# Moving the up projection's weight sums to GpSimd, its Relu and Square to VectorE, and three units' row transfers to GpSimd's queue

## The chip, the cores and the metric

The kernel runs on one core of a Trainium2 chip. The metric is the device time of one execution in microseconds (us). Before the change the median of three runs is 2260.8 us (2259.25 to 2261.42).

## What is computed

One layer of a decoder block on x of shape 1 x 1024 x 1024 in float32. Two token mixers (dilated windowed attention and retention) read the normalised input through one projection, are gated, added, projected (`w_out`) and added to x. Then comes the channel mixer, which the change touches:

```
xn2 = rmsnorm(x, norm2_g)
x   = x + square(relu(xn2 @ w_up)) @ w_down      # w_up 1024 x 4096, w_down 4096 x 1024
```

## The kernel before, in words

**Number format.** Every float32 operand is split into two float32r parts: ScalarE copies it, rounded, into the high part (line 351), and VectorE subtracts that from the original for the low part (line 352). A product takes three matmuls for each pair of tiles: high by high, low by high, high by low (lines 253 to 259).

**The up projection** (lines 1195 to 1311) goes over 16 units j of 256 columns of `w_up`. Each unit is computed by a seven-product scheme of Strassen's kind: products N1 to N7, each of four contractions by three matmuls of 128 x 512, in an order written out by `strassen_order` (line 287): for unit j N6, N5, then N1 of unit j+2, N7, N3, then N2 of unit j+2, N4. `product` (line 400) issues one of them and takes its result away. N6, N7 and N4 accumulate in one and the same bank, whose running content is copied out between them: line 424 (ScalarE) after N6, line 429 (VectorE) after N7.

**The results.** `result` (line 1210) gets the four quarters of a unit's output. Two come in PSUM (`q11`, `q12`, after N2 and N4), two as tiles in SBUF (`u3` after N7, `u2` after N3, made by the subtractions of lines 429 and 434). Each goes through Relu and Square on ScalarE (lines 1219 and 1220). Sums of them (line 1227, VectorE) are the seven operands of the down projection; `put_operand` splits each into a tile `hs` (four buffers) and stores it to `h_d` in HBM from SyncE's queue (line 1237).

**The weights** of a unit come in two raw tiles (line 207, SyncE's queue), of which there are four places: units j and j+2 share theirs. `add_units` (line 125) lists the steps that make the split pieces: A (both halves of the second raw tile) for N1 and N2, D (half of the first) for N4, then the four sums of lines 148 to 151 in the raw tiles on VectorE, then B (second tile) for N6 and N3, C (first tile) for N5 and N7. The list runs A of unit j+1, D, sums, B and C of unit j, then A of unit j+2, and so on. A step is written into the program (`pump`, line 211) as soon as the products that last used its buffer are in it, and a raw tile is loaded anew as soon as the step that used it last (B for the second tile, C for the first) is written.

**The handover.** The operand tiles N1, N5 and N3 of the up projection become the buffers for the rows of `h_d` that the down projection multiplies (`load_rows`, line 1246): a pair of transfers, `xh` and `xl`, of 896 KB each, for every unit u of 32. The rows of u = 0, 1 and 2 are asked for while the last up unit (j = 15) still runs, right after its N1, N5 and N3; all go through SyncE's queue (line 1253). `down` (line 1256) issues the products of the down projection; at the very end GpSimd adds the results into `out` by accumulating transfers (line 1284).

**Order.** Only PE's order is written by hand (line 303). For the other engines and queues a planner sets the order when the program is built: among the instructions that it expects to be ready it takes the one written first. Each engine then works through its list in that order and waits where an operand isn't there. GpSimd's other work is small: row scales (line 366), four-tile differences at the start (line 547), some scalings in attention (line 678).

Of the kernel before, what the change touches and what calls it, by code (L numbers as in the profile page):

```python
# [10 lines left out]
F = mybir.dt.float32  # L11
R = mybir.dt.float32r
AF = mybir.ActivationFunctionType
OP = mybir.AluOpType
# [23 lines left out]
class Weights:  # L38
# [83 lines left out]

                    self.steps.append((self.claim(buf, key), r[need, p], step))

    def add_units(self, tag, srcs):

        base = len(self.src)
        kept = {}
        for s in srcs:
            self.place += [(len(self.src) + i - base) % (self.RAW + 1) for i in range(2)]  # L130
            self.src += [s[0], s[1]]

        def piece(key, buf, r, cols, then=None):
            def step():
                if isinstance(buf, tuple):
                    if not kept:
                        kept["D"] = self.buffer(buf[0])
                    h, l = (x[:, 512 * buf[1]:512 * buf[1] + 512] for x in kept["D"])
                else:
                    h, l = self.buffer(buf)  # L140
                self.split(h, l, self.raw[r][:, cols])
                self.units[key] = h, l
                if then:
                    then()

            self.steps.append((self.claim(buf, key), r, step))

        def sums(r):
            (x22, x21), (x11, x12) = ((self.raw[i][:, 0:512], self.raw[i][:, 512:1024]) for i in (r, r + 1))
            for x, y in ((x22, x21), (x21, x11), (x11, x22), (x12, x11)):  # L150
                self.nc.vector.tensor_tensor(x, x, y, op=OP.add)  # L151

        both = slice(0, 1024)
        for j in range(-1, len(srcs)):
            if j + 1 < len(srcs):
                r = base + 2 * (j + 1)
                piece((tag, j + 1, "A"), self.A[(j + 1) % 2], r + 1, both)
            if j >= 0:
                r = base + 2 * j
                piece((tag, j, "D"), (self.D, j % 2), r, slice(0, 512), lambda r=r: sums(r))  # L160
                piece((tag, j, "B"), self.B[j % 2], r + 1, both, lambda r=r: self.used.add(r + 1))
                piece((tag, j, "C"), self.C, r, both, lambda r=r: self.used.add(r))
        m = len(srcs)
        self.cycle = (0, 1, self.B[m % 2], self.C, self.D, self.B[(m - 1) % 2])
        self.turn = 0
# [135 lines left out]
def hybrid_block(ctx: ExitStack, tc: tile.TileContext, a: dict, out: bass.AP):  # L301
# [72 lines left out]
    for u in range(4):  # L374
# [2 lines left out]
    W.add_tokens("att", [[[a["w_att_q"][u, q, p] for p in range(2)] for q in range(4)] for u in range(len(TOKEN))])  # L377
    NG, NQ = KT, 2 * RH
    W.add_units("in", [a["w_gate_q"][j] for j in range(NG)] + [a["w_rqk_q"][j] for j in range(NQ)]
                + [a["w_gr_q"][j] for j in range(8)])  # L380
    for h in range(RH):
        for u in range(4):
            W.add(a["w_rv"][h, u])
# [6 lines left out]
        for u in range(4):  # L390
            W.add(a["w_out"][nb, u], (4, 5, 2, 3)[u] if nb else (2, 3, 0, 1)[u])
    NU = FF // 256
    W.add_units("up", [a["w_up"][j] for j in range(NU)])
    NC = FF // 512
    W.add_chunks("dn", [[a["w_down"][c, i] for i in range(4)] for c in range(NC)],
                 [{"N1": 0, "N2": 1, "N3": 2, "N5": "n2a", "N7": "n2b", "N6": 5, "N4": 4},
# [798 lines left out]
    with ExitStack() as ph:  # L1195
        up_pool, early, sumst = None, [], ExitStack()
        unit = {}

        def temps():

            nonlocal up_pool
            if up_pool is None:
                assert pipe.slot > last_turn
                norm2.close()
                y0 = pool(sumst, "y0", 1)
                Y.update({r: y0.tile([P, D], F, name=f"Y{r}") for r in (0, 4)})
                up_pool = pool(ph, "p26", 2)
            return up_pool

        def result(j, f, cs, src):  # L1210

            if pipe.slot <= last_turn:
                early.append((j, f, cs, src))
                return
            while early:
                result(*early.pop(0))
            q = "u3" if f and cs.start else "u2" if cs.start else ("q11", "q12")[f]
            r = src if src.space != PSUM else temps().tile([P, 512], F, name=q, bufs=2 if f else 3)
            nc.scalar.activation(r, src, AF.Relu)
            nc.scalar.activation(r, r, AF.Square)  # L1220
            held[j, q] = r
            if q != "u2":
                put_operand(j, {"q11": "N1", "q12": "N2", "u3": "N4"}[q], r)
            sums = {"u2": (("N5", "u3", "u2"), ("N7", "u2", "q11"), ("N6", "q11", "u3")),
                    "q12": (("N3", "q12", "q11"),)}.get(q, ())
            for name, x, y in sums:
                nc.vector.tensor_tensor(held[j, x], held[j, x], held[j, y], op=OP.add)
                put_operand(j, name, held[j, x])

        held = {}  # L1230

        def put_operand(j, name, x):

            hs = temps().tile([P, 2, 512], R, name="hs", bufs=4)
            split(hs[:, 0], hs[:, 1], x)
            dst = h_d[j // 2, :, :, :, DOWN.index(name), j % 2]
            nc.sync.dma_start(dst.rearrange("h t p q -> p (h t) q"),
                              hs.rearrange("p h (t q) -> p (h t) q", q=P).bitcast(F))


        units = [(c, t) for c in range(NC) for t in range(4)]
        rows = {}
        sums = {}
        Y = {}

        def load_rows(u):

            if u < len(units):
                c, t = units[u]
                rows[u] = []  # L1250
                for i, x in enumerate(OP7[("N1", "N5", "N3")[u % 3]]):
                    x = x.rearrange("p a b -> p (a b)")[:, :7 * 2 * P]
                    nc.sync.dma_start(x.bitcast(F), h_d[c, i, t].rearrange("p o k q -> p (o k q)"))
                    rows[u].append(x.rearrange("p (o k q) -> p o k q", o=7, k=2))

        def down(u, name):

            c, t = units[u]
            b = sums.setdefault(u, {})
            bank = BANK[name]  # L1260
            fresh = bank not in b
            if fresh:
                b[bank] = mm.tile([P, 512], F, name="mm")
            o = DOWN.index(name)
            wh, wl = W["dn", c, name]
            xh, xl = rows[u]
            pipe.step(b[bank], [(xh[:, o, k], xl[:, o, k], wh[:, 512 * k:512 * k + 512], wl[:, 512 * k:512 * k + 512])
                                for k in range(2)], None, fresh)
            ps = b[bank]
            lo, hi = halves()  # L1270
            if name == "N1":
                b["b"] = ms.tile([P, 512], F, name="ms")
                nc.scalar.activation(b["b"], ps, AF.Copy, scale=-1.0)  # L1273
            else:
                r, ns, op, last = {"N2": (t, lo, OP.add, True), "N6": (t, hi, OP.subtract, False),
                                   "N5": (t + 4, hi, OP.subtract, False), "N7": (t + 4, hi, OP.add, True),
                                   "N3": (t, hi, OP.add, True), "N4": (t + 4, lo, OP.add, True)}[name]
                begun = c > 0 or name in ("N7", "N3")
                if not begun:
                    nc.scalar.activation(Y[r][:, ns], ps, AF.Copy, scale=1.0 if op == OP.add else -1.0)  # L1280
                else:
                    nc.vector.tensor_tensor(Y[r][:, ns], Y[r][:, ns], ps, op=op)
                if last and c == NC - 1:
                    nc.gpsimd.dma_start(out[r * P:(r + 1) * P, ns], Y[r][:, ns], accum_op=OP.add)
            if t == 3:
                W.free(("dn", c, name))

        for j, name in strassen_order(NU):
            product("up", j, name, unit, OP7, temps, result)
            if j == NU - 1:  # L1290
                if name == "N1":
                    load_rows(0)
                if name == "N2":
                    parts = [x.rearrange("p a b -> p (a b)") for x in OP7[name]]
                    for i, part in enumerate("ab"):
                        W.places["n2" + part] = [x[:, 1024 * i:1024 * i + 1024] for x in parts]
                    W.free(("place", "n2"))
                if name == "N5":
                    load_rows(1)
                if name == "N7":  # L1300
                    down(0, "N1")
                if name == "N3":
                    load_rows(2)
                    down(0, "N2")
        exts.close()
        y1 = pool(sumst, "y1", 1, "right")

        Y.update({r: y1.tile([P, D], F, name=f"Y{r}") for t in (1, 3, 2) for r in (t, t + 4)})
        for x in "abc":
            W.places["y1" + x] = [y1.tile([P, UW], R, name=f"y1{x}{i}") for i in "hl"]  # L1310
        W.free(("place", "y1"))
# [122 lines left out]
```

## Time and profile before

| | before |
|---|---|
| median of the runs (lowest, highest) | 2260.8 us (2259.25, 2261.42) |
| the profiled execution, its span | 2260.28 us, 2258.5 us |
| ScalarE's splits of weight pieces, 128 x 1024, 1680 to 1900 | 1.05 us each |
| VectorE's subtractions of weight pieces, 128 x 1024, 1680 to 1900 | 1.22 us each |
| VectorE's weight sums, 128 x 512 (line 151) | 0.69 us each, 160 in all, 64 of them in the up projection |
| ScalarE's Relu and Square in SBUF (lines 1219, 1220; u) | 32 each, 20.0 and 20.2 us |
| loads of raw weight tiles, 1680 to 1900, issue to landing | 5.1 us in the median |
| row transfers of the down projection (line 1253), issue to landing | 6.4 us in the median |

The page of the profile gives busy times for the whole span; a view by stages gives the same for any stretch, and the view of waits tells who waited for whom. A timeline row has the start, the busy time, engine, line, output and inputs; in square brackets how long the engine sat idle just before and what ended that. In rows of one source line, three durations in ns are the shortest, the median and the longest. Engines: PE is TensorE's matmul, DVE is VectorE, ACT is ScalarE, POOL is GpSimd, SP is SyncE; a q behind the name means the engine's queue of transfers.

### The profile page before, as it was taken

The numbers are of one execution on the slowest core, as the hardware profiler recorded it, in microseconds if no ns is written. First come the engines' busy times: TensorE is split into PE (matmuls) and PEld (weight loads), VectorE is DVE, ScalarE is ACT, GpSimd is POOL, SyncE is SP. The second block draws the span as 40 slices with busy tenths as digits, with TensorE's granted clock in tenths as the row PEclk, the third lists the DMA queues.
The fourth block names the chain that finished last, engine by engine and source line by source line (L and its number), as shares of the span: only waits on it lengthen the run. The fifth ranks groups of instructions, "written<-read, shape, count | busy, mean of one in ns | idle before, by whom it ended". The sixth has DMA issues, their size and how long they took to land.

```text
span 2258.5 us, 28527 instructions
## 1 busy us (share of the span) xinstructions
PE 2189.5 (97%) x10064; PEld 1794.3 (79%) x10064; DVE 1432.1 (63%) x2543; ACT 1103.3 (49%) x1934; POOL 194.1 (9%) x180
## 2 busy tenths in 40 slices
PE   8999999999999999989999999999999999899998
PEld 6788788888888887878888788888787777688887
DVE  6766676455655666557867741544867778676863
ACT  6433453577744477545545522113666667522210
POOL 3314453000000000000000000000000000000002
PEclk9999999999999999999999999999999999999999
DMA  6443534454555445455333583553388779966657
GB/s 197 131 126 112 150 93 123 154 161 146 172 151 166 153 151 162 127 177 153 119 89 115 165 284 126 187 177 134 109 232 229 231 225 284 313 243 249 244 221 172
DMA packets 346559, 392.77 MB, mean 174 GB/s; under 512 B 34737, under 2 KB 271921, under 8 KB 346162
## 3 DMA queue, kind: packets, MB, share of 16 engines
q1 hardware_dynamic: 344114, 386.77, 54.7%
q0 software_dynamic: 2304, 4.20, 1.3%
q8 instruction: 79, 1.29, 0.2%
q14 instruction: 62, 0.51, 0.1%
HBM read 252.39 MB, written 138.51 MB: 173 GB/s over the span
## 4 chain that ended last, share of the span: by engine, by line
PE 71%; DVE 8%; DMA 8%; ACT 6%; issue 4%; POOL 3%; SPq 0%; POOLq 0%; ACTq 0%; DVEq 0%
PE mm L254 41%; PE ms L254 24%; DMA raw<-in_w_up 2%; ACT wh L351 2%; DVE wl L352 2%; DMA h_d<-hs 2%; PE tr L787 1%; PE tr L806 1%; DVE raw L151 1%; DVE hs L352 1%; DMA xl<-h_d 1%; POOL x L547 1%; DMA raw<-in_w_att_q 1%; DVE xl L352 1%; PE tr L645 1%
## 5 line engine op out<-in xcount | busy, mean ns | idle before, releaser
L352 DVE TENSOR_TENSOR wl<-raw,wh 128x1024 fp32r<-128x1024 f32 (+1 forms) x292 | 332.4, 1139 | 231.5 <-ACT wh L351 229.8
L351 ACT ACTIVATE wh<-raw 128x1024 fp32r<-128x1024 f32 (+1 forms) x292 | 287.1, 986 | 321.3 <-PE ms L254 110.5
L254 PE MATMUL mm<-xh,wh 128*128 128x512 f32 x896 | 346.3, 410 | 0.0
L254 PE MATMUL mm<-xl,wh 128*128 128x512 f32 x896 | 329.0, 390 | 1.7 <-DVE xl L352 1.7
L254 PE MATMUL mm<-xh,wl 128*128 128x512 f32 x768 | 300.7, 392 | 0.0
L254 PE MATMUL mm<-wh,xh 128*128 128x512 f32 x736 | 297.8, 405 | 2.3 <-ACT ms L1273 2.3
L254 PE MATMUL mm<-wh,xl 128*128 128x512 f32 x736 | 289.3, 393 | 4.0 <-DMA xl<-h_d 4.0
L254 PE MATMUL mm<-wl,xh 128*128 128x512 f32 x736 | 288.0, 391 | 0.0
L254 PE MATMUL ms<-xh,wh 128*128 128x512 f32 x544 | 228.2, 419 | 15.3 <-ACT u L424 13.4
L254 PE MATMUL ms<-xl,wh 128*128 128x512 f32 x544 | 213.6, 393 | 0.7 <-DVE xl L352 0.7
L254 PE MATMUL ms<-xh,wl 128*128 128x512 f32 x544 | 213.6, 393 | 0.0
L254 PEld LDWEIGHTS mm<-xh,wh 128*128 128x128 f32 x896 | 168.9, 189 | 32.5 <-ACT u L427 0.4
L254 PEld LDWEIGHTS mm<-xl,wh 128*128 128x128 f32 x896 | 169.0, 189 | 31.6 <-DVE xl L352 2.1
L254 PEld LDWEIGHTS mm<-xh,wl 128*128 128x128 f32 x768 | 144.3, 188 | 31.4
L254 PEld LDWEIGHTS mm<-wh,xl 128*128 128x128 f32 x736 | 138.9, 189 | 35.3 <-DMA xl<-h_d 4.9
L254 PEld LDWEIGHTS mm<-wh,xh 128*128 128x128 f32 x736 | 139.2, 189 | 28.8 <-ACT ms L1273 3.2
L254 PEld LDWEIGHTS mm<-wl,xh 128*128 128x128 f32 x736 | 139.5, 189 | 26.0
L254 PE MATMUL ms<-wh,xh 128*128 128x512 f32 x336 | 137.1, 408 | 6.7 <-DVE c L700 4.4
L254 PEld LDWEIGHTS ms<-xh,wh 128*128 128x128 f32 x544 | 102.9, 189 | 40.8 <-ACT u L424 18.5
L254 PE MATMUL ms<-wh,xl 128*128 128x512 f32 x336 | 132.8, 395 | 2.5 <-DVE xl L352 2.5
L254 PE MATMUL ms<-wl,xh 128*128 128x512 f32 x336 | 132.3, 394 | 1.0 <-DVE ss L365 0.8
L254 PEld LDWEIGHTS ms<-xh,wl 128*128 128x128 f32 x544 | 102.7, 189 | 22.5
(282 smaller groups left out, 3809.9 us busy)
## 6 DMA issues: line engine op xcount, KB each, us to landing
h_d<-hs SPq DMA_DIRECT2D x112, 512.0 KB, 5.6
xh<-h_d SPq DMA_DIRECT2D x32, 896.0 KB, 4.9
xl<-h_d SPq DMA_DIRECT2D x32, 896.0 KB, 6.9
raw<-in_w_att_q SPq DMA_DIRECT2D x48, 512.0 KB, 4.3
raw<-in_w_up SPq DMA_DIRECT2D x32, 512.0 KB, 5.0
raw<-in_w_down SPq DMA_DIRECT2D x32, 512.0 KB, 5.2
qk_d<-T SPq DMA_DIRECT2D x48, 256.0 KB, 3.5
raw<-in_w_gate_q SPq DMA_DIRECT2D x16, 512.0 KB, 4.5
```

The lines of the kernel that those rows point to most:

```text
L151: self.nc.vector.tensor_tensor(x, x, y, op=OP.add)
L254: self.nc.tensor.matmul(ps, x, y, start=start, stop=stop, skip_group_check=not first)
L351: nc.scalar.activation(dst_h, src, AF.Copy)
L352: nc.vector.tensor_tensor(dst_l, src, dst_h.bitcast(F), op=OP.subtract)
L547: nc.gpsimd.tensor_tensor(x[v], x[v], x[u], op=op)
L645: nc.tensor.transpose(pt[:, i, :], c[:, i * P:(i + 1) * P], ident)
L787: nc.tensor.matmul(sp[:, :w], q[:, e * P:(e + 1) * P], k[:, k0 * P:k0 * P + w], start=True, stop=True)
L806: nc.tensor.matmul(po[:, :DH], st["t"][:, j * P:(j + 1) * P], v[:, k0 + j, :], start=(j == 0), stop=(j == nk - 1))
```

## The change

The weight sums of the up projection are issued on GpSimd (those of the input projection stay on VectorE). Results that are in SBUF (`u2` and `u3`) get Relu and Square from one VectorE instruction, max(r, 0) * r, in place; those in PSUM stay with ScalarE. The row transfers of the first three down units are issued from GpSimd's queue instead of SyncE's.

```diff
-    def add_units(self, tag, srcs):
+    def add_units(self, tag, srcs, adder):
...
             for x, y in ((x22, x21), (x21, x11), (x11, x22), (x12, x11)):
-                self.nc.vector.tensor_tensor(x, x, y, op=OP.add)
+                adder.tensor_tensor(x, x, y, op=OP.add)
...
-                + [a["w_gr_q"][j] for j in range(8)])
+                + [a["w_gr_q"][j] for j in range(8)], nc.vector)
...
-    W.add_units("up", [a["w_up"][j] for j in range(NU)])
+    W.add_units("up", [a["w_up"][j] for j in range(NU)], nc.gpsimd)
...
-            nc.scalar.activation(r, src, AF.Relu)
-            nc.scalar.activation(r, r, AF.Square)
+            if src.space != PSUM:
+                nc.vector.scalar_tensor_tensor(r, src, 0.0, src, op0=OP.max, op1=OP.mult)
+            else:
+                nc.scalar.activation(r, src, AF.Relu)
+                nc.scalar.activation(r, r, AF.Square)
...
-                    nc.sync.dma_start(x.bitcast(F), h_d[c, i, t].rearrange("p o k q -> p (o k q)"))
+                    (nc.gpsimd if u < 3 else nc.sync).dma_start(x.bitcast(F), h_d[c, i, t].rearrange("p o k q -> p (o k q)"))
```

## The prediction

> **What bounds the kernel now.** I read the page's busy shares first, then the stages, then the waits of the one stage that the change touches, then one pass of that stage on each engine.
>
> ```profile
> span 2258.5 us, 28527 instructions
> PE 2189.5 (97%) x10064; PEld 1794.3 (79%) x10064; DVE 1432.1 (63%) x2543; ACT 1103.3 (49%) x1934; POOL 194.1 (9%) x180
> 1680.00:1900.00 220.00, 209.08 (x904) 169.54 (x902) 163.70 (x228) 145.57 (x236) 0.00 (x0) 0.99 0.83 238
> 1900.00:1960.00 60.00, 53.52 (x220) 42.45 (x219) 42.51 (x55) 37.52 (x60) 0.00 (x0) 0.94 1.02 329
> ACT wh L351 <- DMA raw<-in_w_up: 42.9, 10, 5.7
> PEld ms L254 <- ACT u L424: 15.1, 10, 2.6
> PE ms L254 <- ACT u L424: 10.8, 9, 2.2
> ```
>
> TensorE is busy 97% of the span, so the change can only take or give the rest. In the stage table (PE first, then PEld, DVE, ACT, POOL, the granted clock, the DMA share) the up projection loses 220 - 209.1 = 10.9 us of PE between 1680 and 1900, and its handover to the down projection 6.5 us up to 1960. GpSimd stands idle there. The waits from 1680 to 1900 say that all of PE's loss has one releaser, ScalarE's copy of line 424, nine times. ScalarE itself waits ten times for a weight load, 4.3 us each. One pass shows why; ScalarE first, then PE, VectorE and SyncE.
>
> ```profile
> 1751.52 1.06 ACT L351 ACTIVATE wh<-raw 128x1024 fp32r<-128x1024 f32 x1 [4.08 <-DMA raw<-in_w_up]
> ...
> 1759.93 0.62 ACT L351 ACTIVATE wh<-raw 128x512 fp32r<-128x512 f32 x1
> ...
> 1764.70 1.06 ACT L351 ACTIVATE wh<-raw 128x1024 fp32r<-128x1024 f32 x1 [1.62 <-DVE raw L151]
> ...
> 1771.54 1.06 ACT L351 ACTIVATE wh<-raw 128x1024 fp32r<-128x1024 f32 x1 [3.80 <-DMA raw<-in_w_up]
> ```
> ```profile
> 1761.61 0.50 PE L254 MATMUL ms<-xh,wh 128*128 128x512 f32 x1 [0.95 <-ACT u L424]
> ```
> ```profile
> 1752.61 1.23 DVE L352 TENSOR_TENSOR wl<-raw,wh 128x1024 fp32r<-128x1024 f32 x1 [3.56 <-ACT wh L351]
> 1753.76 0.68 DVE L434 TENSOR_TENSOR u<-mm,u 128x512 f32<-128x512 f32 x1
> 1754.46 0.69 DVE L352 TENSOR_TENSOR hs<-u,hs 128x512 fp32r<-128x512 f32 x1
> 1755.80 0.69 DVE L1227 TENSOR_TENSOR u<-u,u 128x512 f32<-128x512 f32 x1 [0.65 <-ACT u L1220]
> ...
> 1760.59 0.69 DVE L352 TENSOR_TENSOR wl<-raw,wh 128x512 fp32r<-128x512 f32 x1 [0.24 <-ACT wh L351]
> 1761.31 0.69 DVE L151 TENSOR_TENSOR raw<-raw 128x512 f32<-128x512 f32 x1
> 1762.04 1.42 DVE L151 TENSOR_TENSOR raw<-raw,raw 128x512 f32<-128x512 f32 x2
> 1763.38 0.68 DVE L352 TENSOR_TENSOR hs<-q,hs 128x512 fp32r<-128x512 f32 x1
> 1763.98 0.68 DVE L151 TENSOR_TENSOR raw<-raw 128x512 f32<-128x512 f32 x1
> ...
> 1765.79 1.23 DVE L352 TENSOR_TENSOR wl<-raw,wh 128x1024 fp32r<-128x1024 f32 x1 [0.52 <-ACT wh L351]
> ```
> ```profile
> 1767.04 0.34 SPq L207 DMA_DIRECT2D raw<-in_w_up  x1
> ```
>
> Read them as a **ring of four legs**, from one split of a weight piece A to the next. Leg a: from A's split at 1751.52 through VectorE's work up to the end of D's split (1760.59 + 0.69 = 1761.28), 9.76 us. Leg b: the four weight sums, until B's split begins at 1764.70, 3.42 us. Leg c: B's split, to 1767.02, 2.32 us. Leg d: only now is that raw tile free, the load goes out at 1767.04 and lands at 1771.54, 4.52 us. Together 20.02 us. PE needs less for a unit: seven products of twelve matmuls, at 904 matmuls in 209.1 us of busy time 84 x 0.2313 = 19.4 us (an estimate from that row, a little high, since records can be missing). So the ring sets the pace. PE feels it through line 424: N7 accumulates into the bank that line 424 must first have copied, and that copy stands in ScalarE's queue behind A's split.
>
> **The change, part by part.** The sums of leg b go to GpSimd. Its only big two-input additions here are those of line 547, of the same shape.
>
> ```profile
> L547 POOL TENSOR_TENSOR x<-x,x x16: 1258/1454/2235, 21.5 to 71.2; 128x512 f32<-128x512 f32 x16
> ```
> ```profile
> 38.94 4.68 POOL L547 TENSOR_TENSOR x<-x,x 128x512 f32<-128x512 f32 x3
> ...
> 67.64 5.24 POOL L547 TENSOR_TENSOR x<-x,x 128x512 f32<-128x512 f32 x3 [2.76 <-ACT x L535]
> ```
> ```profile
> 39.67 2.82 DVE L352 TENSOR_TENSOR xl<-x,xh 128x512 fp32r<-128x512 f32 x2
> ...
> 43.73 0.68 DVE L352 TENSOR_TENSOR xl<-x,xh 128x512 fp32r<-128x512 f32 x1
> ```
>
> The shortest addition takes 1.26 us; beside VectorE three take 4.68 or 5.24, 1.56 or 1.75 each, and VectorE's two subtractions of two SBUF operands take 2.82 us there instead of 2 x 0.68. The two engines hold each other up. In leg b VectorE will have just such work (the hs subtraction at 1763.38 and the sum of line 1227). Four sums therefore cost from 4 x 1.258 = 5.03 to 4 x 1.75 = 7.0 us; I take 4 x 1.5 = 6.0, between the median 1.454 and the first of the triples. **Leg b grows by 6.0 - 3.42 = 2.6 us** (ends +1.6 and +3.6). On VectorE, 4 x 0.69 = 2.8 us a unit go, but they go from leg b, not from leg a.
>
> The Trainium skill, SBUF — State Buffer, section "Who interferes with whom", has it that a VectorE instruction with two SBUF inputs and a GpSimd one that reads SBUF exclude each other for a whole instruction. The triples agree in kind (extra time on both sides); by the rule in full, with three of VectorE's instructions let in between four sums, leg b would be 5.03 + 3 x 0.69 = 7.1 us; I stay at 6.0, by the rows.
>
> Relu and Square of the two SBUF results become one VectorE instruction each, so ScalarE loses four instructions a unit and VectorE gains two.
>
> ```profile
> L1219 ACT ACTIVATE u<-u x22: 612/624/636, 1691.5 to 1892.5; 128x512 f32<-128x512 f32 x22
> L1220 ACT ACTIVATE u<-u x22: 631/632/635, 1692.2 to 1893.2; 128x512 f32<-128x512 f32 x22
> L1188 DVE SCALAR_TENSOR_TENSOR xn<-xr,ssq,g x8: 742/745/747, 1555.6 to 1605.2; 128x512 f32<-128x512 f32 x8
> ```
>
> ScalarE is freed of 2 x (0.62 + 0.63) = 2.5 us. But leg a is VectorE's: between 1752.61 and 1761.28 it idles only 0.65 us (for the Square) and 0.24 us. The new instruction for u2 sits in that gap, 0.75 us by line 1188, and nothing that it replaces was VectorE's. So leg a gains 0.89 - 0.75 = 0.1 us if the order stays. The instruction for u3 has no price: it follows line 429, while VectorE waits 3.3 to 3.6 us for A. More can come from the order, which is not written by hand for these engines: A now comes later against PE, so that hs of u3, line 434 and the new instruction of u2 (0.69 + 0.68 + 0.75 = 2.1 us), which need nothing of A, can be put before A's subtraction instead of behind it. This trace can't show it; between 0 and 2.1 I take half, 1.05. **Net for a pass: +2.6 - 0.1 - 1.05 = about +1.4 us** (ends: 1.6 - 0.1 - 2.1 = -0.6, and 3.6 - 0.1 = +3.5).
>
> How many passes: the first and last A of those ten waits are here, from the chain of work in order of time.
>
> ```profile
> 1670.24 1.07 ACT wh L351
> ...
> 1874.22 1.07 ACT wh L351
> ```
>
> That is 10 passes of 20.4 us, and two earlier ones (units 3 and 4) that PE had slack for and will have less; I count 12 passes. 12 x 1.4 = **+17 us**. The sums of units 0 and 1 run beside the second norm, where GpSimd also makes the row scales; VectorE is relieved, GpSimd's queue gets longer; I put it at 0, with 3 us either way.
>
> The rows of the first three down units: today SyncE issues them behind the stores of hs.
>
> ```profile
> 1931.61 0.90 SPq L1253 DMA_DIRECT2D xh<-h_d  x1
> ...
> 1939.56 1.15 SPq L1253 DMA_DIRECT2D xl<-h_d  x1
> ```
> ```profile
> 1948.20 0.80 PE L254 MATMUL mm<-wh,xl 128*128 128x512 f32 x1 [3.59 <-DMA xl<-h_d]
> ```
> ```profile
> 1948.00:1952.00 4.00, 3.80 (x9) 3.03 (x10) 0.00 (x0) 0.58 (x1) 0.00 (x0) 0.50 1.00 319
> ```
> ```profile
> L1284 POOL DMA_DIRECT2D out<-Y x16: 856/866/1062, 2213.5 to 2251.6; - x16
> ```
> ```profile
> 1893.81 1.66 SPq L1253 DMA_DIRECT2D xh<-h_d  x1
> ```
> ```profile
> 1901.62 0.69 DVE L151 TENSOR_TENSOR raw<-raw 128x512 f32<-128x512 f32 x1
> ```
>
> xl of unit 2 goes out 8 us after xh and PE waits 3.6 us for it; then the granted clock is 0.50 for a stretch, 9 matmuls where 17 or 18 fit, about 2 us more. On GpSimd's queue xl follows xh at once. A transfer of 256 KB costs GpSimd 0.87 us to issue; these have 896 KB, so from 0.87 to 3.0 us each (by size), six in all. Queued behind them can be only the sums of unit 15: the first row transfers waited for N1 of unit 15 until 1893.8, those sums began at 1901.6, so they fit even at 3.0 each. SyncE loses six issues that blocked the stores. But the DMA share is 1.02 in this stage, so landing stays slow, and the rows of unit 3, still with SyncE, are next late. I take 4 of the 5.6 us: **-4 us** (ends 0 and -6.5).
>
> Sum: the profiled execution took 2260.28 us (span 2258.5, and 1.8 around it); 2260.3 + 17 - 4 = 2273. The median of the runs shown is 2260.8, half a us above; **2274 us**.
>
> **Rivals.**
> - *The order bends to the slower sums* (the other side). If all 2.1 us of leg a move ahead of A's subtraction and the sums stay near 1.26 us each, a pass shrinks by 0.6 us: 12 x 0.6 + 4 = 11 less, 2249 us. If D's subtraction is also placed ahead of two hs subtractions (another 1.4), the ring is shorter than PE's own unit, all of PE's 10.9 us go and up to 6.5 at the handover: 2243. I name 2246 us. It decides where what leaves leg a is as much as leg b gains, 2.6 us. For it: ScalarE is freed of 2.5 us a unit, and its queue is what PE waits for. Against: leg a is VectorE's, without gaps.
> - *The port fills up.* Nothing is reordered, and every sum meets VectorE: +3.5 us a pass, 12 x 3.5 - 4 = +38: 2298 us. For it: the triple at 67.64. VectorE's 163.7 of 220 us is 15.1 us a unit; less 2.8, plus 1.5, with 5 to 6 us of additions that exclude it, it is 19 to 20, as long as PE's unit. The skill's rule above would lead here.
> - *Both parts cancel.* The pass grows by 0.4 and the handover gives 5: 2260 us.
>
> **How the numbers follow.** Forecast (2265 to 2285) 0.43, port 0.20, cancel 0.13, the bent order 0.24. About 0.2%, 4.5 us, is what a measurement can tell from no change, so slower 0.63, same 0.13, faster 0.24. The likeliest case's own range is 2265 to 2285; the range for 8 in 10 leaves out the lower half of the bent order and the upper edge of the port case: 2249 to 2299.
>
> **What would show it.** In the changed profile: sums of line 151 on GpSimd at 1.4 to 1.75 us; ScalarE's wait for them before B's split up from 1.62 us to about 4 in a pass; A's splits 21 to 22 us apart; PE's idle time still released by line 424; VectorE's hs subtractions beside the sums stretched above 0.69. For the handover: no wait of PE for xl near the third unit. I am wrong if A's splits come 19 to 20 us apart, if PE's waits move to another releaser, or if GpSimd's issues of rows hold up the sums of unit 15.

## The result, and the profile after

The changed kernel takes **2313.7 us** in the median of six runs (2310.68 to 2317.79), the kernel before 2261.0 us (2259.25 to 2262.04) beside it: 1.0234 times as long, 95% interval 1.0221 to 1.0248. The forecast was 2274 us, in a range of 2249 to 2299. The direction was right and the size was not: 53 us were lost, where 13 were forecast.

Lines behind 1218 of the changed kernel stand three higher: line 1227 of before is 1230, 1237 is 1240, 1253 is 1256, 1273 is 1276, 1280 is 1283, 1282 is 1285; the VectorE instruction for relu and square is line 1220, Relu and Square on ScalarE are 1222 and 1223. First the page, busy time and share of the span:

```profile
span 2316.0 us, 28525 instructions
...
PE 2213.4 (96%) x10064; PEld 1812.8 (78%) x10064; DVE 1446.2 (62%) x2511; ACT 1068.4 (46%) x1870; POOL 295.6 (13%) x250
```

PE works no less than before, but it waits more. The stages (PE, PEld, DVE, ACT, POOL, granted clock, DMA share, GB/s) say where:

```profile
1600.00:1640.00 40.00, 30.06 (x122) 23.43 (x121) 33.68 (x42) 21.69 (x37) 14.92 (x10) 0.83 0.22 73
```
```profile
1680.00:1900.00 220.00, 192.99 (x786) 155.31 (x785) 148.63 (x180) 106.75 (x168) 55.49 (x39) 0.94 0.73 206
1900.00:1960.00 60.00, 52.56 (x210) 42.13 (x209) 41.77 (x50) 29.59 (x47) 18.75 (x14) 0.91 0.77 228
```

From 1600 to 1640 PE is busy for 30.06 us, where it was 36.47. In the 220 us from 1680 on PE did 904 matmuls before and does 786 now, and the granted clock of that stage is 0.94 instead of 0.99. The waits of the same stretch (us in total, times, longest):

```profile
ACT wh L351 <- POOL raw L151: 44.5, 10, 4.5
ACT wh L351 <- DMA raw<-in_w_up: 35.9, 9, 4.5
...
PE mm L254 <- ACT u L427: 27.0, 10, 4.3
```

PE's wait has **another releaser**: line 427, the copy of u3, and no longer line 424. One pass shows how. ScalarE first, then PE, VectorE, GpSimd, SyncE:

```profile
1767.68 0.58 ACT L1222 ACTIVATE q<-ms 128x512 f32<-128x512 f32 x1
1768.16 0.62 ACT L351 ACTIVATE wh<-raw 128x512 fp32r<-128x512 f32 x1
...
1775.75 1.06 ACT L351 ACTIVATE wh<-raw 128x1024 fp32r<-128x1024 f32 x1 [4.52 <-POOL raw L151]
1776.72 0.61 ACT L351 ACTIVATE hs<-q 128x512 fp32r<-128x512 f32 x1
1777.23 0.58 ACT L427 ACTIVATE u<-mm 128x512 f32<-128x512 f32 x1
...
1784.36 1.06 ACT L351 ACTIVATE wh<-raw 128x1024 fp32r<-128x1024 f32 x1 [3.70 <-DMA raw<-in_w_up]
```
```profile
1777.87 0.50 PE L254 MATMUL mm<-xh,wh 128*128 128x512 f32 x1 [2.40 <-ACT u L427]
```
```profile
1762.59 1.23 DVE L352 TENSOR_TENSOR wl<-raw,wh 128x1024 fp32r<-128x1024 f32 x1 [2.71 <-ACT wh L351]
...
1768.92 0.68 DVE L352 TENSOR_TENSOR wl<-raw,wh 128x512 fp32r<-128x512 f32 x1
1771.27 1.62 DVE L352 TENSOR_TENSOR hs<-q,hs 128x512 fp32r<-128x512 f32 x1 [1.67 <-ACT hs L351]
1772.92 1.66 DVE L1230 TENSOR_TENSOR q<-q,q 128x512 f32<-128x512 f32 x1
1776.84 1.23 DVE L352 TENSOR_TENSOR wl<-raw,wh 128x1024 fp32r<-128x1024 f32 x1 [2.26 <-ACT wh L351]
```
```profile
1769.68 1.29 POOL L151 TENSOR_TENSOR raw<-raw 128x512 f32<-128x512 f32 x1 [17.28 <-DVE wl L352]
1771.05 2.98 POOL L151 TENSOR_TENSOR raw<-raw,raw 128x512 f32<-128x512 f32 x2
1774.11 1.61 POOL L151 TENSOR_TENSOR raw<-raw 128x512 f32<-128x512 f32 x1
```
```profile
1767.22 11.84 SPq L1240 DMA_DIRECT2D h_d<-hs  x6
1779.15 2.36 SPq L207 DMA_DIRECT2D raw<-in_w_up  x2
```

From A's subtraction at 1762.59 to the end of D's at 1769.60 VectorE has no gap. The four sums take from 1769.68 to 1775.72. Until then ScalarE stands still at the head of its list (4.52 us) with the copy of line 427 two places behind. And a new wait is at the end: B's low part is ready at 1776.84 + 1.23 = 1778.07, which frees the raw tile, but the load goes out at 1779.15 only, because a store of hs stands in front of it in SyncE's queue.

The table measures the legs in each kernel as in the prediction: a from the start of A's split to the end of D's subtraction, b from there to B's split, c to the end of B's subtraction, then the wait until the load is issued, then until the next A's split. It has the means, in us, of the passes from one A to the next that begin between 1660 and 1900.

| kernel (passes) | a | b | c | d: to the issue | d: to A | pass |
|---|---|---|---|---|---|---|
| before (10) | 9.64 | 3.42 | 2.32 | 0.03 | 4.99 | 20.40 |
| sums alone (11) | 9.32 | 6.38 | 2.31 | 0.60 | 4.49 | 23.11 |
| relu alone (10) | 9.96 | 3.42 | 2.32 | 0.03 | 5.23 | 20.96 |
| rows alone (10) | 9.67 | 3.42 | 2.32 | 0.03 | 4.97 | 20.41 |
| all, the change (10) | 8.29 | 6.15 | 2.31 | 1.08 | 5.50 | 23.34 |

No leg of the changed kernel holds a wait for PE, so PE's lower clock is not what makes the pass longer.

Following the same instruction through both profiles, unit by unit, gives the places of the loss. The changed kernel's profile is 8.7 us late already at 1515 us, before anything changed (more on that at the end). Up to the subtraction of line 429 after N7 of unit 0, 7.9 us are added, which is the start beside the second norm; from unit 0 to unit 15 38.7 us (2.58 a unit, where the passes of the table lose 2.94: the units at both ends lose less); from there to the steady part of the down projection 2.3 us. That is 48.9 us, against forecasts of 0, +17 and -4.

### The profile page after: what moved, and what is told of

Read it like the earlier page. It is cut to its first block, busy times and chain, and to the rows that moved or that the text cites. A ratio compares the mean times of both kernels' runs of the same rounds, so it can differ in the third digit from the quotient of the medians.

```text
span 2316.0 us, 28525 instructions
## 1 busy us (share of the span) xinstructions
PE 2213.4 (96%) x10064; PEld 1812.8 (78%) x10064; DVE 1446.2 (62%) x2511; ACT 1068.4 (46%) x1870; POOL 295.6 (13%) x250
## 3 DMA queue, kind: packets, MB, share of 16 engines
q8 instruction: 79, 1.29, 0.2%
## 4 chain that ended last, share of the span: by engine, by line
PE 68%; issue 14%; POOL 6%; DVE 4%; DMA 4%; ACT 3%; SPq 0%; POOLq 0%; ACTq 0%; DVEq 0%
PE mm L254 39%; PE ms L254 23%; POOL raw L151 4%; PE tr L787 1%; PE tr L806 1%; DMA raw<-in_w_att_q 1%; DVE wl L352 1%; POOL x L547 1%; PE tr L645 1%; DMA pa_d<-s 1%; ACT wh L351 1%; PE ms L928 1%; PE tr L799 1%; POOL out L1287 1%; PE tr L984 1%
## 5 line engine op out<-in xcount | busy, mean ns | idle before, releaser
L254 PE MATMUL mm<-xh,wh 128*128 128x512 f32 x896 | 356.0, 421 | 35.7 <-ACT u L427 35.4
L254 PE MATMUL mm<-xl,wh 128*128 128x512 f32 x896 | 337.5, 400 | 4.7 <-DVE xl L352 4.7
L254 PE MATMUL mm<-xh,wl 128*128 128x512 f32 x768 | 308.2, 401 | 0.0
L254 PEld LDWEIGHTS mm<-xh,wh 128*128 128x128 f32 x896 | 173.8, 194 | 75.2 <-ACT u L427 41.1
L254 PEld LDWEIGHTS mm<-xl,wh 128*128 128x128 f32 x896 | 173.9, 194 | 36.0 <-DVE xl L352 5.2
L254 PEld LDWEIGHTS mm<-xh,wl 128*128 128x128 f32 x768 | 149.3, 194 | 33.4
L961 POOL TENSOR_TENSOR st<-st,half 128x1 f32<-128x1 f32 x32 | 25.1, 786 | 877.4 <-PE ms L254 599.9
```

The lines of the kernel that those rows point to most:

```text
L254: self.nc.tensor.matmul(ps, x, y, start=start, stop=stop, skip_group_check=not first)
L961: nc.gpsimd.tensor_tensor(st[:, 9:10], st[:, 8:9], half[:, 0:1], op=OP.pow)
```

## The experiments

The **ring theory** says that a pass lasts as long as the four legs, so that the sums' longer time is paid in every unit, wherever it makes PE wait. The rivals: the loss is a matter of ScalarE's list (line 427 behind a blocked split); GpSimd holds VectorE up at the SBUF port; the parts of the change only hurt together.

### One part at a time

Each kernel is the changed one with other parts set back: the first line for the sums, the second for relu and square, the third for the rows.

```diff
-    W.add_units("up", [a["w_up"][j] for j in range(NU)], nc.gpsimd)
+    W.add_units("up", [a["w_up"][j] for j in range(NU)], nc.vector)
...
-            if src.space != PSUM:
+            if False:
...
-                    (nc.gpsimd if u < 3 else nc.sync).dma_start(x.bitcast(F), h_d[c, i, t].rearrange("p o k q -> p (o k q)"))
+                    nc.sync.dma_start(x.bitcast(F), h_d[c, i, t].rearrange("p o k q -> p (o k q)"))
```

Sums alone. 

> The kernel before with one part alone: the up projection's weight sums on GpSimd. Ring theory (the sums sit on the ring of legs, so their extra time is paid in every pass): leg b +2.7 us as in the changed kernel, 12 passes, 32 us, and some 8 us where the sums of units 0 and 1 run beside the second norm: 2261 + 40 = 2301 us. Rival, the parts hurt together (a bent order on ScalarE and SyncE that the relu part brings): the sums alone cost leg b less than the slack of the rest, 2261 to 2275 us.

Relu alone. 

> The kernel before with one part alone: relu and square of SBUF results as one VectorE instruction. Ring theory: leg a shorter by 0.1 to 1.65 us a pass, leg b as before, so PE's idle time of 10.9 us shrinks: 2250 to 2260 us. Rival (this part is what puts stores ahead of the raw load on SyncE, leg d +1.8 us): 12 x 1.8 = 22 us slower, 2283 us.

Rows alone. 

> The kernel before with one part alone: the rows of the first three down units issued by GpSimd. As predicted: the 3.6 us wait for xl and the low clock behind it go, 4 us faster, 2257 us. Rival (the DMA engines are full there, so the earlier rows only push back the raw loads and the stores): 0 to 3 us slower, 2261 to 2264 us.

Relu and rows, without the sums. 

> The changed kernel with the sums back on VectorE (relu and rows stay changed). If the sums are the whole loss, and the two other parts give what was forecast for them: 2250 to 2257 us. If relu and rows have a share in the loss (leg d, handover): 2265 to 2285 us.

| kernel | median, us | ratio to before | 95% interval |
|---|---|---|---|
| sums alone | 2303.39 | 1.0186 | 1.0169 to 1.0203 |
| relu alone | 2268.62 | 1.0030 | 1.0019 to 1.0040 |
| rows alone | 2265.88 | 1.0019 | 1.0009 to 1.0028 |
| relu and rows | 2274.0 | 1.0060 | 1.0046 to 1.0073 |

Of 2261 us these ratios are +42, +6.8, +4.3 and +13.6 us. The three parts add up within what the intervals allow: 42 + 6.8 + 4.3 = 53.1, and the whole change lost 53. So the parts do not need each other to hurt, **none of them helps**, and the sums are four fifths of it. Relu came out between its two forecasts, the rows slower than both of theirs.

*Relu* loses by the leg that it was to shorten. ScalarE is freed, but it was not what leg a waited for, and the planner puts the instructions into another order:

```profile
1757.60 1.06 ACT L351 ACTIVATE wh<-raw 128x1024 fp32r<-128x1024 f32 x1 [3.94 <-DMA raw<-in_w_up]
1758.57 0.62 ACT L351 ACTIVATE hs<-u 128x512 fp32r<-128x512 f32 x1
```
```profile
1759.21 0.69 DVE L352 TENSOR_TENSOR hs<-u,hs 128x512 fp32r<-128x512 f32 x1 [3.21 <-ACT hs L351]
1759.82 1.22 DVE L352 TENSOR_TENSOR wl<-raw,wh 128x1024 fp32r<-128x1024 f32 x1
```

An hs subtraction now stands ahead of A's in VectorE's list, but its own copy stands behind A's split in ScalarE's. So A's subtraction begins 2.22 us after A's split began (1757.60 to 1759.82), where before it was 1.09 (1751.52 to 1752.61). Leg a is 0.32 us longer in the mean, the next A's split comes 0.24 us later behind its load, and the pass grows by 0.56 us.

*Rows* leave the passes alone and lose at the handover. GpSimd, then SyncE, ScalarE and PE of the kernel with the rows alone:

```profile
1894.71 0.78 POOL L1256 DMA_DIRECT2D xl<-h_d  x1 [288.52 <-PE mm L254]
1895.48 0.58 POOL L1256 DMA_DIRECT2D xh<-h_d  x1
```
```profile
1895.48 16.24 SPq L1240 DMA_DIRECT2D h_d<-hs  x6
```
```profile
1902.14 1.06 ACT L351 ACTIVATE wh<-raw 128x1024 fp32r<-128x1024 f32 x1 [3.81 <-DMA raw<-in_w_down]
...
1906.84 0.63 ACT L351 ACTIVATE hs<-q 128x512 fp32r<-128x512 f32 x1 [1.60 <-DMA h_d<-hs]
1907.38 0.58 ACT L424 ACTIVATE u<-ms 128x512 f32<-128x512 f32 x1
```
```profile
1944.22 0.63 ACT L351 ACTIVATE hs<-u 128x512 fp32r<-128x512 f32 x1 [5.20 <-DMA h_d<-hs]
...
1953.21 0.59 ACT L1283 ACTIVATE Y<-mm 128x512 f32<-128x512 f32 x1
```
```profile
1908.01 0.79 PE L254 MATMUL ms<-xh,wh 128*128 128x512 f32 x1 [5.25 <-ACT u L424]
```
```profile
1953.36 0.80 PE L254 MATMUL ms<-xh 128*128 128x512 f32 x1 [11.34 <-ACT Y L1283]
```

The issue costs GpSimd 0.54 to 0.78 us, no more. But both transfers of a unit now go out together, and the slowest of the stores of hs issued from 1890 to 1950 takes longer to land. The shortest, median and longest time, with the rows alone and before:

```profile
DMA to landing us min/median/max: 3.2/5.8/14.8
```
```profile
DMA to landing us min/median/max: 4.2/5.9/9.1
```

ScalarE waits for what lands late, first 3.81 us for a raw tile of `w_down` and 1.60 us for an hs buffer to come free, later 5.20 us and three shorter times for such buffers; its copies of lines 424 and 1283 stand behind that, and PE waits 5.25 and 11.34 us for them. The wait for xl is gone, and a longer one has come.

### The start

```diff
-                adder.tensor_tensor(x, x, y, op=OP.add)
+                (self.nc.vector if tag == "up" and r - base < 4 else adder).tensor_tensor(x, x, y, op=OP.add)
```

> The changed kernel with the sums of units 0 and 1 back on VectorE; those of the other 14 units stay on GpSimd. The eight sums beside the second norm cost 8.3 us by the trace (the step between the last row of the norm and the first product of the up projection): 2314 - 8 = 2306 us. If that step is only put off until unit 2's sums: 2312 us or more.

Measured: 2302.95 us, 1.0194 times before (1.0175 to 1.0212), against 1.0234 for the whole change: 0.4%, 9 us. The step at the norm's last row is gone. What made it, in the changed kernel, GpSimd, VectorE and PE:

```profile
1605.04 2.93 POOL L151 TENSOR_TENSOR raw<-raw,raw 128x512 f32<-128x512 f32 x2
1607.93 3.39 POOL L151 TENSOR_TENSOR raw<-raw 128x512 f32<-128x512 f32 x2
1611.28 4.49 POOL L151 TENSOR_TENSOR raw<-raw,raw 128x512 f32<-128x512 f32 x2
```
```profile
1605.10 1.75 DVE L1188 SCALAR_TENSOR_TENSOR xn<-y,ssq,g 128x512 f32<-128x512 f32 x1 [0.44 <-POOL ssq L366]
...
1610.11 4.51 DVE L352 TENSOR_TENSOR wl<-raw,wh 128x1024 fp32r<-128x1024 f32 x2
```
```profile
1610.24 0.79 PE L254 MATMUL mm<-xl,wh 128*128 128x512 f32 x1 [4.73 <-DVE xl L352]
```

Seven of the eight sums of units 0 and 1 run back to back here, and every VectorE instruction with two inputs in SBUF that begins between 1605 and 1616 is stretched: line 1188 from 0.74 to 1.75 us, a 128 x 1024 subtraction from 1.22 to 2.26. Here VectorE, not GpSimd, is what PE waits for.

### Is it a ring?

The kernel before without the up projection's sums.

```diff
-            for x, y in ((x22, x21), (x21, x11), (x11, x22), (x12, x11)):
+            for x, y in () if tag == "up" else ((x22, x21), (x21, x11), (x11, x22), (x12, x11)):
```

> The kernel before without the up projection's weight sums: this work is left out, so the pieces B and C are split from unsummed weights. If the legs really form a ring that sets the pace, leg b falls from 3.42 to about 0.7 us, the ring (20.7 us) to 18, below PE's own 19.4, and PE's 10.9 us of idle time go: 2250 us. If the raw tile isn't what the pace hangs on and only the queue order is: no change, 2261 us.

Measured: 2242.93 us, 0.9932 times before (0.9915 to 0.9950), a gain of 15 us. The same stage:

```profile
1680.00:1900.00 220.00, 220.00 (x972) 182.15 (x972) 147.20 (x197) 159.26 (x254) 0.00 (x0) 1.00 0.89 256
```
```profile
ACT wh L351 <- PE ms L254: 20.6, 12, 1.9
```

PE has no gap left, and from unit 1 to unit 12 each unit takes 19.04 us: that is PE's own time, a little under the 19.4 estimated. So the sums were on the path in the kernel before. The run also takes 2.8 us a unit off VectorE, so by itself it doesn't tell the ring from VectorE's load; the third buffer below does. In the wait row a split waits for PE. It is the split of a piece of 128 x 1024. It waits for a product that sums in ms, so the piece is C: C has one buffer, and N7, the last to read it, sums there.

```profile
1746.20 1.06 ACT L351 ACTIVATE wh<-raw 128x1024 fp32r<-128x1024 f32 x1 [1.91 <-PE ms L254]
```

With the sums gone it is PE that sets the pace of the splits. The split of D (128 x 512) waits for PE neither here nor, from 1660 on, in the kernels before and after the change. It stands in ScalarE's list right behind the Relu of N4's result (1767.68 and 1768.16 in the pass above), and N4 of the unit two before had ended 3.6 us earlier (7.4 us in the kernel before, at 1759.93). D's two buffers put it there all the same: its step is written into the program only when that N4 is in it.

### The list of ScalarE, or the ring?

Piece B's copy goes from ScalarE to VectorE, so that line 427 no longer stands behind a split that waits for sums.

```diff
-                self.split(h, l, self.raw[r][:, cols])
+                (self.split_v if key[0] == "up" and key[2] == "B" else self.split)(h, l, self.raw[r][:, cols])
```

> The changed kernel with one instruction a unit moved: the copy of piece B's split goes from ScalarE to VectorE, behind the same sums. Queue theory (the loss comes in because ScalarE stands still for 4.5 us at the head of its queue, waiting for GpSimd's sums, with the copy of line 427, for which PE waits, behind it): PE's 35 us of waits for line 427 go and 20 to 30 us come back, 2284 to 2294 us. Ring theory (the late load of the raw tile sets the pace): legs keep their lengths, VectorE has one more instruction of about 0.6 to 1.2 us, and the time stays, 2308 to 2320 us.

Measured: 2311.63 us, 1.0232 times before (1.0206 to 1.0259), against 1.0234. The wait for line 427 is gone, and PE waits elsewhere:

```profile
ACT hs L351 <- DVE q L1230: 50.4, 10, 5.1
...
DVE wh L372 <- POOL raw L151: 25.5, 10, 2.6
...
PE mm L254 <- ACT ms L419: 20.7, 10, 2.4
...
PE ms L254 <- ACT u L424: 4.5, 6, 1.2
```

So line 427 as such is not the cause: the releaser that a profile names can be moved without a gain. The queue theory in its wider form is not refuted by this run: VectorE's list now stands still for the sums in ScalarE's place (25.5 us), ScalarE waits behind it for an operand (50.4 us), and the copy of line 419 stands behind that. But the legs are nearly as long as before (8.28, 5.84, 2.43, 1.08 and 5.25 us, a pass of 22.88), and a pass can't be shorter than its legs, whatever PE waits for by name.

### The late load

The up projection's loads from unit 2 on go out on GpSimd's queue, where no store stands ahead of them.

```diff
-        self.nc.sync.dma_start(raw[:, :self.src[n].shape[1]], self.src[n])
+        (self.nc.gpsimd if n in self.aside else self.nc.sync).dma_start(raw[:, :self.src[n].shape[1]], self.src[n])
```

> The changed kernel with the up projection's weight loads (from unit 2 on) issued by GpSimd instead of SyncE, so that no store of hs stands in front of them. Ring theory: the 1.0 us by which the load goes out late in every pass goes, less up to 0.8 us that GpSimd takes for an issue: 2 to 12 us faster, 2302 to 2312 us. If the late issue is slack, no change; if GpSimd's issues hold up its sums, slower than 2314 us.

Measured: 2346.64 us, 1.0391 times before (1.0375 to 1.0408). The issue comes 0.40 us after the tile is free instead of 1.08, and legs b and c stay (6.12 and 2.31). But leg a goes from 8.29 to 11.58 us: the planner, which knows the new queue, puts C's subtraction and both VectorE instructions for relu and square between A's split and D's. The pass is 26.05 us. The pass grows with its legs, but the run does not show the late issue by itself. The kernel with the sums alone shows it side by side: there the load goes out late (1.08 us) in every other pass. The six late passes between 1660 and 1900 take 24.17 us in the mean, the five others (0.03 us) 21.84. In the late ones the time from the issue to A's split is longer too, 5.10 against 3.77 us; that the late issue is what makes it longer is not shown.

### Taking the sums off the ring

D gets a third buffer (units 5 to 14), so that its split and the sums need not come behind N4 of the unit two before. The 4 KB come from the fourth hs buffer; a control has three hs buffers and nothing else.

```diff
-                    h, l = (x[:, 512 * buf[1]:512 * buf[1] + 512] for x in kept["D"])
+                    h, l = self.third() if buf[1] == 2 else (x[:, 512 * buf[1]:512 * buf[1] + 512] for x in kept["D"])
...
-                piece((tag, j, "D"), (self.D, j % 2), r, slice(0, 512), lambda r=r: sums(r))
+                piece((tag, j, "D"), (self.D, j % (3 if tag == "up" and 4 < j < 15 else 2)), r, slice(0, 512), lambda r=r: sums(r))
...
-            hs = temps().tile([P, 2, 512], R, name="hs", bufs=4)
+            hs = temps().tile([P, 2, 512], R, name="hs", bufs=3)
```

On the kernel before. 

> The kernel before with a third buffer for piece D in the up projection (units 5 to 14), so that D's split, and with it the sums, needn't wait until N4 of the unit two before has been read; its 4 KB a partition are taken from the fourth hs buffer. Ring theory: D's split can follow A's at once, leg a falls from 9.6 us to 4 or less, the ring is shorter than PE's 19.04 us a unit, and about 10 passes gain 1.2 to 1.6 us: 2245 to 2250 us. Rival (the missing hs buffer makes ScalarE wait for stores, which costs as much): 2258 to 2275 us; the control run without the third buffer tells the two apart.

The control. 

> Control for the third buffer of D: the kernel before with three hs buffers in place of four and nothing else. The store of a buffer must land before ScalarE writes it again, so waits for it grow from 6.4 us (of ScalarE, 1680 to 1900): 2262 to 2275 us.

On the changed kernel. 

> The changed kernel with the third buffer for piece D and three hs buffers. If the sums cost their time because they lie on the ring, a shorter leg a pays for them: leg a falls from 8.1 us to 4 or 5, the pass from 23.3 to 20 or less, 10 passes give 30 us: 2280 to 2290 us, plus what the control shows for the buffer. If GpSimd's sums cost by holding up VectorE at the SBUF port, the pass stays at 22 to 23.3 us: 2300 to 2314 us.

| kernel | median, us | ratio to before | 95% interval |
|---|---|---|---|
| before with D's third buffer | 2244.49 | 0.9922 | 0.9907 to 0.9937 |
| control, three hs buffers | 2264.15 | 1.0014 | 1.0004 to 1.0023 |
| the change with D's third buffer | 2294.75 | 1.0148 | 1.0133 to 1.0163 |

**The first of these beats both kernels**, by 16 us (0.8%) and 69 us. In the passes from 1754 on, with the third buffer in turn, leg a is 2.92 us instead of 9.64. VectorE works more than before in this stage (175.62 us, where it was 163.70), and PE is full all the same:

```profile
1680.00:1900.00 220.00, 218.01 (x960) 179.59 (x959) 175.62 (x246) 159.83 (x254) 0.00 (x0) 1.00 0.91 261
```

The last one is the most telling. It has the sums on GpSimd, as slow as ever. Four units of it, and a unit's sums in them:

```profile
1783.00:1861.00 78.00, 77.56 (x339) 62.97 (x338) 69.26 (x77) 45.68 (x74) 26.75 (x16) 1.00 0.86 243
```
```profile
1810.09 1.30 POOL L151 TENSOR_TENSOR raw<-raw 128x512 f32<-128x512 f32 x1 [12.43 <-DVE wl L352]
1811.47 3.85 POOL L151 TENSOR_TENSOR raw<-raw,raw 128x512 f32<-128x512 f32 x2
1815.40 1.62 POOL L151 TENSOR_TENSOR raw<-raw 128x512 f32<-128x512 f32 x1
```

The sums take 1810.09 to 1817.02, 6.9 us, longer than in the changed kernel (6.0), and VectorE is busy 69.26 of 78 us. Yet PE is busy 77.56 of 78, and from unit 6 to unit 12 a unit takes 19.3 to 19.7 us, where it was 23.3; PE's own time is 19.04. The order shows why. D's split now stands ahead of A's (1808.67 and 1809.71), and the raw tiles of the two had landed at 1806.08 and 1808.98, 2.6 and 0.7 us before. In the changed kernel A's split waits for its tile in every pass; here neither does, so the ring has slack. By the trace the loss that is left, 1.5%, comes from the start (7 us), from the units up to 5, before the third buffer is in turn (22 us), and from the last three (7 us), and the units between gain 8 us on the kernel before. With the control's 4 us the time is at the upper end of what was expected. So neither GpSimd's pace nor VectorE's stretched instructions cost more than 0.3 to 0.7 us a unit there: **the sums cost what they add to the ring, and next to nothing where the ring has slack.** For these units that settles the port rival.

### The third unit's rows alone

```diff
-                    nc.sync.dma_start(x.bitcast(F), h_d[c, i, t].rearrange("p o k q -> p (o k q)"))
+                    (nc.gpsimd if u == 2 else nc.sync).dma_start(x.bitcast(F), h_d[c, i, t].rearrange("p o k q -> p (o k q)"))
```

> The kernel before with the rows of the third down unit alone issued by GpSimd (the two transfers for which PE waited 3.6 us); those of the first two units stay with SyncE between the stores. The step of the prediction by itself: 4 us faster, 2257 us. If the bytes and not the queue are short there, other waits take its place: 2261 to 2266 us.

Measured: 2260.06 us, 0.9990 times before (0.9978 to 1.0002). No difference that can be told: the interval reaches from 5 us faster to half a us slower, so it does not exclude the 4 us that the prediction gave this step either.

## Why the prediction was wrong, point by point

- **What bounds it: right.** The ring does set the pace: without the sums PE has no gap, and with the third buffer for D the sums on GpSimd cost next to nothing. Leg a is VectorE's, as forecast: in the changed kernel VectorE has no gap in it. What the prediction did not see is why D's split stands at the end of that leg: D's two buffers put it behind N4, and a third one takes leg a from 9.64 to 2.92 us in the kernel before.
- **Leg b, +2.6 forecast, +2.73 measured (3.42 to 6.15): right.** The first two sums of a unit take 1.29 us each, those beside VectorE 1.6. Four at 1.29 and the 0.35 us of gaps around them make 5.51, so of the 2.73 us some 2.1 are GpSimd's own pace and about 0.6 the two engines' holding each other up; this split is worked out from rows and was not tried alone.
- **Leg a, -0.1 and -1.05 forecast, -1.35 measured (9.64 to 8.29): right** for the change as a whole, but not by the sum of its parts: relu alone lengthens it by 0.32, the sums alone shorten it by 0.32. The half of 2.1 us taken for the order was a choice, and it came near: hs of u3 and line 434 went ahead of A's subtraction (1781.05, 1782.51 and 1785.45 in the pass shown), the instruction for u2 stayed behind it.
- **Legs c and d, which the sum of the pass leaves at nothing: leg d is the step that failed in the pass.** Leg c stayed (2.32 and 2.31). Leg d grew by 1.05 us to the issue of the load and by 0.51 from there to A's split. B's split had slid to where the next store of hs stands ahead of the load in SyncE's queue. The prediction weighed the order of ScalarE's and VectorE's lists, and did not ask what SyncE's list would do. A pass of the steady stretch costs 2.94 us instead of 1.4.
- **The count, 12 passes: too few.** The loss runs from unit 0 to unit 15, 15 steps of 2.58 us, and the first of them already loses 1.4. Together: 38.7 us instead of 17.
- **The start, 0 with 3 us either way: wrong, +8 to 9 us.** "VectorE is relieved" looked at VectorE's count of instructions and not at their length: beside seven sums in a row each with two inputs in SBUF takes 1.75 us and more. The triples of line 547 quoted in the prediction had shown this, and were used for the price of the sums only.
- **The handover, -4: wrong, +2.3 in the trace and +4.3 us for the rows alone.** The wait for xl went, as forecast; that the 4 us follow from it was wrong for all three units' rows, and for the third unit's rows alone it stays open. The DMA share of 1.02 in that stage was quoted, and its consequence drawn for landing only: the stores of hs pay, ScalarE waits for an hs buffer, and PE waits for ScalarE.
- **"PE's idle time still released by line 424": wrong**, it is line 427; the prediction had named this as a sign of being wrong, but with the split of B on VectorE the releaser changes and the time does not.
- **The rivals.** The port case gave 2298 us, nearest to the result, for a reason that the runs refute for the passes (leg b took 6.15 us and not 7.0, and the other growth is leg d's) and confirm for the start. The Trainium skill, SBUF — State Buffer, section "Who interferes with whom", has it that a VectorE instruction with two SBUF inputs contends with a GpSimd instruction that reads SBUF, and that their shared port pair is an exclusive lock. In kind the trace agrees: beside the sums 0.69 us of VectorE become 1.62 and 1.66, and sums of 1.29 become 1.6. The prediction's 7.1 us by that rule counted three of VectorE's instructions between the sums. In the pass shown two stand there, which makes 5.03 + 2 x 0.69 = 6.4 us, nearer to the 6.15 measured.

The failed terms add up: 21.7 us too little for the passes, 7.9 for the start, 6.3 for the handover, 35.9 in all, and the forecast of +13 with these is the 48.9 us of the traces. The medians have 53 us; the rest lies within what single profiles differ by.

## What to carry to other kernels

Before moving work to a slower engine, find the loop that it lies on (here: split, sums, split, load of the buffer freed by it) and ask for that loop's slack; the same sums cost 42 us in a loop without slack and next to nothing a unit in one with it, and one buffer more for the piece that ends the loop's longest leg gained 16 us where the moves to other engines lost. When a leg shifts in time, look at every list that it crosses, those of the transfers too: what was issued at once may now find a store ahead of it. And where the DMA engines are already full, as here at a share of 1.02, issuing transfers earlier can just choose who waits.

## What the runs showed of the hardware that was not expected

- Beside the sums a 128 x 512 subtraction takes 1.62 to 1.77 us instead of 0.69, a sum beside it 1.6 to 1.7 instead of 1.29: there VectorE loses more than GpSimd. Beside 128 x 1024 subtractions, which go from 1.22 to 2.26 us, two sums take 4.49 us, and both lose alike. One instruction with a single input in SBUF (line 1180, at 1616.24) took 0.68 us beside a sum, as long as alone. The instruction for relu and square, both inputs the same SBUF tile, takes 0.68 us, as long as a plain two-input one.
- GpSimd issues a transfer of 896 KB in 0.54 to 0.78 us, less than the 0.87 us that it took for 256 KB with accumulation at the end of the kernel.
- Single profiles of one and the same program part differ by several us. All kernels here issue the same instructions for the first 1515 us; against the profile of before they arrive there 0.2 to 8.7 us later (the changed kernel 8.7, the kernel with the third unit's rows 6.8, though its time is that of before). Differences between two profiles were therefore taken from that point on, and the verdicts from the medians. The profile of before is not typical everywhere even so: four kernels whose handover is issued as before (sums alone, relu alone, no sums, three hs buffers) come from unit 15 to the steady part 1.3 to 5.6 us faster than it does. So the handover's loss of 2.3 us may be several us too small.
